# Two-layer hybrid decoder trunk on one core: activation tables loaded by name, and plain products for the last two output tiles of each FFN

## The chip, the core and the metric

The kernel runs on one core of a Trainium2 chip. TensorE multiplies, VectorE (DVE) and GpSimd (POOL) work elementwise, ScalarE (ACT) evaluates functions and copies, and SyncE (SP) starts transfers between HBM and the on-chip memory. PSUM banks hold what TensorE gives out, one bank for 128x512 numbers. The metric is the device time of one execution in microseconds (us), the median of several runs.

## What is computed

Two decoder layers work on 1024 tokens of width 1024, in float32. Each layer adds the result of an attention and then that of a gated FFN (2816 hidden columns) to its input, each behind an RMS norm; a last RMS norm ends it.

```python
def rmsnorm(x, g):
    return x * lax.rsqrt(jnp.mean(x * x, -1, keepdims=True) + EPS) * g

def swiglu(h, w_gate, w_up, w_down):
    return (jax.nn.silu(h @ w_gate) * (h @ w_up)) @ w_down

def reference(x, ...):
    for layer in range(2):
        h = rmsnorm(x, attn_norm[layer])
        x = x + (even_mixer if layer == 0 else mla_mixer)(h, ...)
        x = x + swiglu(rmsnorm(x, ffn_norm[layer]), ...)
    return rmsnorm(x, final_norm)
```

The first layer's mixer has a stick-breaking attention (its weights come from sigmoids) and a sliding-window attention (softmax); the second layer's is a latent attention (softmax) behind low-rank projections with norms of their own.

## The kernel before

Activations lie transposed: tiles of 128 features by 512 tokens, so each tensor has two token halves. Every float32 operand is split into a high and a low part (`split_w` for weights, `split_act`, `split` for activations): ScalarE copies the high part, VectorE subtracts it from the original. A product is then three matmuls of 128x128 by 128x512 (`mm3`).

**The norms.** `square_sum` collects squares of the tiles of one half in two or three partial sums (ScalarE squares; VectorE and GpSimd add). `rstd` sums them over the features with matmuls against a matrix of ones, takes Ln and Exp(-0.5 x) on ScalarE and refines the result with four operations on VectorE, the last three in a chain behind Exp. Nothing in the code says which activation table these functions use; a pass over the finished program places a table load ahead of an activation whenever the table that is loaded last does not serve it. It places one ahead of Ln, one ahead of Exp and one ahead of Silu or Sigmoid that follow.

**The FFN.** It uses seven instead of eight block products for a 2x2 block product (a fast scheme of Strassen's kind). The blocks are two halves of the features by two token halves (A, B): `FORMS` names the seven sums of activation blocks, B11, B21, T2, T1, T3, B22 and N4; B11 and B21 are blocks of half A, B22 one of half B, and T1, T2, T3, N4 are differences. `forms` loads the weight blocks and forms the matching weight sums on GpSimd (`combine`, `sub`). At the beginning of an FFN only half A's norm is at hand, so six pairs of column tiles first make the products of B11 and B21 alone (kind "plain"), gate and up in turn; Silu is applied to the first. Meanwhile half B's norm is taken, and `combinations` forms T1, T2, T3, N4 and B22 from the tiles of both halves, a piece after each product. The other products follow pair by pair (`outputs`); the four result blocks c11, c12, c21 (named u) and c22 of each pair give the forms of the down projection (`combine`), which are stored to HBM (`keep`).

The down projection runs in three chunks of 4, 4 and 3 column pairs, and within a chunk over four groups j of two output tiles each. A group has seven products of n tiles; each product's result is added to some of the four residual tiles (x11, x12, x21, x22; 11 additions and a copy in all). In the last chunk (`end`) a tile that is finished goes to `Last.add`, which squares it for the next norm and, at the end of the kernel, starts the last norm of a half as soon as its eight tiles are there. The last group of the last chunk (j == 3) uses the order `LATE`, with weight sums of kind "late"; there B's tiles are finished after the fourth and the fifth product, A's after the sixth and the seventh.

**What sets the order.** Only TensorE in the first attention is ordered by hand. Everywhere else a scheduler orders each engine's instructions by a model of times, and the engines run their queues in that order. TensorE's sums for a norm stand in its queue like any other matmul.

Of the kernel before, what the change touches and what calls it, by code (L numbers as in the profile page):

```python
# [10 lines left out]
F32 = mybir.dt.float32  # L11
# [20 lines left out]
FORMS = ("B11", "B21", "T2", "T1", "T3", "B22", "N4")  # L32
LATE = ("B11", "T2", "T1", "T3", "B22", "B21", "N4")

# [37 lines left out]
class Kernel:  # L72
# [98 lines left out]
    def forms(self, mats, twins=None):  # L171
# [3 lines left out]


        nc = self.nc
        sub = lambda o, x, y: nc.gpsimd.tensor_tensor(o, x, y, ALU.subtract)  # L178
        turns = {"fast": (0, 1, 0, 4, 2, 1, 3), "late": (0, 0, 4, 2, 0, 1, 3), "rest": (0, 4, 2, 1, 3)}
        flat = [(i, j) for i, m in enumerate(mats) for j in range(len(turns.get(m[0], m[1])))]  # L180
# [24 lines left out]
        def prep():  # L205
            i, j = flat[len(ready)]
            kind, _, n = mats[i]
            early = twins is not None and i == twins[1]
            if j == (6 if early else 0):
                for x in (i, i + 1):  # L210
                    if x < len(mats) and x not in raws:
                        load(x)
            t = raws[i]
            if kind == "rest" and j == 0:
                combine(t, n)
                sub(t[1][:, :n], t[1][:, :n], t[0][:, :n])
            ready.append(self.split_w(t[turns[kind][j] if kind in turns else j], n))
            if kind not in ("fast", "late"):
                return
            if j == (1 if kind == "fast" else 0):  # L220
                combine(t, n)
            if j == 1:
                a11, a12 = t[0][:, :n], t[1][:, :n]
                sub(a12 if kind == "fast" else a11, a12, a11)

# [39 lines left out]
    def stat_acc(self, accs, src, k):  # L265

        nc = self.nc
        out = self.tmp("acc" if len(accs) < 2 else "sq")
        if k in (1, 3, 7):
            nc.gpsimd.tensor_tensor(out, src, src, ALU.mult)  # L270
        else:
            nc.scalar.activation(out, src, AF.Square)
        if len(accs) < 2:
            accs.append(out)
            return
        eng = nc.gpsimd if k in (2, 4) else nc.vector
        eng.tensor_tensor(accs[k % 2], accs[k % 2], out, ALU.add)

    def rstd(self, r, accs, n, scale=1.0, eps=None, eps_out=None, tag="mm"):
# [67 lines left out]
    def norm_in(self, xsrc, g0, pool, tag, split=False, hook=None):  # L347
        act = [[None, None] for _ in range(NT)]
        rs = []
        for hf in range(2):  # L350
# [9 lines left out]
            if split:  # L360
                for k in range(NT):
                    self.stat_acc(accs, srcs[k], k)
            rs.append(self.rstd(self.tl(pool, [P, HALF], F32, tag, 2), accs if split else self.merge(accs), D,
                                tag="t" if split else "mm"))
# [206 lines left out]
    def swa_steps(self, mi, kbox, vbox, qbox, done):  # L571
# [4 lines left out]
        def score(b):  # L576
# [14 lines left out]
            for h in range(2):  # L591
                for i, k in enumerate((kh, kl)):
# [6 lines left out]
                                           ALU.mult, ALU.add)  # L599
            nc.vector.tensor_reduce(st, pt[:, :, o:], AX.X, ALU.max, negate=True)  # L600
            for h in range(2):
                nc.scalar.activation(pt[:, h, o:], pt[:, h, o:], AF.Exp, bias=st[:, h:h + 1],
                                     accum_out=box["s", b // 4][:, h, b % 4:b % 4 + 1])
# [323 lines left out]
    def ffn(self, layer, xt, rs, accs, first, last):  # L927
# [9 lines left out]
        add = lambda o, x, y: nc.vector.tensor_tensor(o, x, y, ALU.add)  # L937
        F = {n: [None] * 4 for n in FORMS}
        self.slot = {n: n for n in FORMS}
        NP = NHID // 2  # L940
        NA = 6
# [8 lines left out]
        def down_mat(p0, n, j):  # L950
            d = lambda m, h: dw[m][:, (h * NP + p0) * P:(h * NP + p0 + n) * P]
            kind = "late" if p0 + n == NP and j == 3 else "fast"
            return (kind, (d(2 * j, 0), d(2 * j, 1), d(2 * j + 1, 0), d(2 * j + 1, 1)), n * P)
# [68 lines left out]
        for i in range(NA):  # L1022
            for g in range(2):
                u, c = [self.tl(self.rp, [P, HALF], F32, "lone", 3) for _ in range(2)]
                nc.scalar.copy(u, p("B11"))
                keep(u, f"U{g}", i)
                add(c, u, p("B21"))
                if g == 0:
                    nc.scalar.activation(c, c, AF.Silu)
                    sil = c  # L1030
# [3 lines left out]
                if i == 0 and g == 0:  # L1034
                    rs[B] = self.rstd(self.tl(self.rp, [P, HALF], F32, "rr", 2), self.acc_list(accs[B]), D)
                    self.tctx.close()
# [7 lines left out]
        with self.pool("tc", side="right") as self.tp:  # L1044
            t = lambda tag: self.tl(self.tp, [P, HALF], F32, tag)
            def outputs(i, g, sil):
# [33 lines left out]
                add(c12, c12, p("B22"))  # L1080
                done(c12, 2)
                yield
# [42 lines left out]
        for c, (p0, n) in enumerate(chunks):  # L1125
# [4 lines left out]
            for j in range(4):  # L1130
                m1, m2 = 2 * j, 2 * j + 1
                x11, x12, x21, x22 = xt[m1][A], xt[m1][B], xt[m2][A], xt[m2][B]
                u = self.tl(self.tp, [P, HALF], F32, "u", 2)
                for name in LATE if end and j == 3 else FORMS:
                    ps = self.any_bank()
# [24 lines left out]
                    if j == 3 and not end:  # L1160
                        build(name, *chunks[c + 1], (self.tp, [P, HALF], F32, "ld", 8))

    def rope_tables(self, tp):
# [419 lines left out]
class Last:  # L1583
# [12 lines left out]
    def open(self):  # L1596
        self.ctx.callback(self.k.wctx.close)
        self.k.set_nsq(5 if self.final else 3)
        self.pool = self.k.tp = self.ctx.enter_context(self.k.pool("st", side="right"))
# [120 lines left out]
```

## Time and profile before

| | |
|---|---|
| median of 3 runs | 2467.93 us (2467.6 to 2468.2) |
| the profiled execution, its own time | 2461.47 us |
| its span, first to last instruction | 2459.7 us |
| instructions | 33726 |
| matmuls | 11242 |
| activation table loads in the built order | 35 |

The profile is of one execution. Times in its rows count from the start of its span. The page gives each engine's busy time; further views list groups of instructions by line, the busy time in stretches, and the instructions in order of time. A row in order of time gives the start, the duration, the engine, the line, the operation with output and inputs, and in brackets how long the engine sat idle before it and whose result ended that. The operations of `rstd` have lines 285 (sum), 289 (Ln behind the matmuls), 290, 296 (Exp), 297, 298 and 299.

### The profile page before, as it was taken

To read this page: it belongs to the slowest core of one execution; us is meant where nothing else is said; L and a number is where in the kernel's file an instruction comes from. 1 tells how busy PE (TensorE), PEld (TensorE's weight loads), DVE (VectorE), ACT (ScalarE), POOL (GpSimd) and SP (SyncE) were. 2 spreads that over 40 slices of the span, in tenths; PEclk is the share of its full clock that TensorE was granted. 3 is DMA by queue.
4 is the path that set the end of the run, shared out by engine and by line. 5 is a ranking of instruction groups with operands and counts; after the bars stand their busy time and mean duration, and the time that the engine had idled before them with its cause. 6 is when DMAs were issued, how large, how long until landed. Compare 5 with 4: busy or idle time off the path is not lost. (4 is left out here: it accounts for less than half of the span.)

```text
span 2459.7 us, 33726 instructions
## 1 busy us (share of the span) xinstructions
PE 2311.8 (94%) x11242; PEld 1901.9 (77%) x11242; DVE 1916.6 (78%) x2854; ACT 1229.4 (50%) x2462; POOL 975.7 (40%) x786
## 2 busy tenths in 40 slices
PE   7999999889999999999988999999889999999996
PEld 5877787777788887778666888887768888877784
DVE  7777777678577668889877888885587876788988
ACT  6555566554223334335655788774453233343453
POOL 6333323215976444333233223321035663434333
PEclk8999999999999999999999999999999999999998
DMA  3011236644354236454333111235235442354531
GB/s 130 22 39 44 66 123 202 210 137 152 116 185 150 98 105 196 141 154 133 113 117 107 50 57 53 65 134 197 86 113 171 157 166 95 107 173 144 175 104 69
DMA packets 167130, 298.65 MB, mean 121 GB/s; under 512 B 20675, under 2 KB 29356, under 8 KB 166956
## 3 DMA queue, kind: packets, MB, share of 16 engines
q1 hardware_dynamic: 166956, 296.51, 37.2%
q8 instruction: 88, 1.44, 0.2%
q14 instruction: 86, 0.70, 0.1%
HBM read 216.10 MB, written 81.38 MB: 121 GB/s over the span
## 5 line engine op out<-in xcount | busy, mean ns | idle before, releaser
L145 ACT CAST whi<-wa 128x512 fp32r<-128x512 f32 (+1 forms) x422 | 255.5, 607 | 447.1 <-PE mm L238 99.7
L146 DVE TENSOR_TENSOR wlo<-wa,whi 128x512 fp32r<-128x512 f32 (+1 forms) x422 | 344.7, 817 | 69.4 <-ACT whi L145 68.9
L178 POOL TENSOR_TENSOR wa<-s,wa 128x512 f32<-128x512 f32 (+1 forms) x66 | 93.4, 1416 | 258.8 <-DVE wlo L146 230.7
L201 POOL TENSOR_TENSOR s<-wb,wb 128x512 f32<-128x512 f32 (+1 forms) x66 | 93.8, 1421 | 200.3 <-DVE wlo L146 147.3
L1472 PE MATMUL z<-mk,mq 128*128 128x512 f32 (+2 forms) x576 | 146.9, 366 | 11.0 <-ACT w L1485 10.4
L146 DVE TENSOR_TENSOR wlo<-wb,whi 128x512 fp32r<-128x512 f32 (+1 forms) x136 | 133.6, 983 | 27.5 <-ACT whi L145 27.4
L145 ACT CAST whi<-wb 128x512 fp32r<-128x512 f32 (+1 forms) x136 | 82.3, 605 | 140.6 <-PE d L238 42.0
L1485 ACT ACTIVATE w<-z,st 128x512 f32<-128x512 f32 (+3 forms) x192 | 110.7, 582 | 35.2 <-DVE st L1481 25.3
L237 PE MATMUL mm<-hh,whi 128*128 128x512 f32 x304 | 124.2, 409 | 1.3 <-ACT whi L145 1.3
L1478 DVE TENSOR_REDUCE st<-z 128x1 f32<-128x512 f32 (+1 forms) x192 | 104.1, 550 | 25.6 <-PE z L1472 17.9
L178 POOL TENSOR_TENSOR wa<-wa,wa 128x512 f32<-128x512 f32 (+1 forms) x68 | 105.6, 1552 | 44.1 <-issue 26.9
L238 PE MATMUL mm<-hl,whi 128*128 128x512 f32 x304 | 122.4, 403 | 0.0
L239 PE MATMUL mm<-hh,wlo 128*128 128x512 f32 x304 | 121.5, 400 | 0.0
L399 DVE TENSOR_TENSOR ptl<-t,pth 128x512 fp32r<-128x512 f32 x160 | 108.1, 683 | 16.1 <-ACT pth L398 14.7
L936 POOL TENSOR_TENSOR c<-c,c 128x512 f32<-128x512 f32 x66 | 101.6, 1552 | 26.0 <-DVE c L1054 22.6
L1472 PEld LDWEIGHTS z<-mk,mq 128*128 128x128 f32 x576 | 92.7, 192 | 24.5 <-ACT w L1485 16.0
L178 POOL TENSOR_TENSOR wb<-wa,wb 128x512 f32<-128x512 f32 (+1 forms) x68 | 99.5, 1463 | 28.9 <-DMA c<-a 12.8
L398 ACT CAST pth<-t 128x512 fp32r<-128x512 f32 x160 | 91.0, 590 | 17.1 <-PE t L395 8.2
L403 PE MATMUL mm<-pth,v 128*128 128x256 f32 x320 | 93.8, 309 | 2.5 <-ACT pth L398 2.3
L395 PE MATMUL t<-ident,w 128*128 128x128 f32 x576 | 94.7, 276 | 1.3 <-ACT w L1485 1.2
L403 PE MATMUL mm<-ptl,v 128*128 128x256 f32 x320 | 87.2, 297 | 1.0 <-DVE ptl L399 1.0
L712 DVE TENSOR_TENSOR ptl<-t,pth 128x512 fp32r<-128x512 f32 x80 | 54.4, 683 | 41.9 <-ACT pth L711 41.5
(535 smaller groups left out, 7619.0 us busy)
## 6 DMA issues: line engine op xcount, KB each, us to landing
a<-c SPq DMA_DIRECT2D x120, 256.0 KB, 2.9
ld<-a SPq DMA_DIRECT2D x98, 256.0 KB, 3.4
wa<-w_gate SPq DMA_DIRECT2D x68, 256.0 KB, 2.7
wa<-w_up SPq DMA_DIRECT2D x68, 256.0 KB, 2.7
lone<-a SPq DMA_DIRECT2D x56, 256.0 KB, 3.3
wb<-w_gate SPq DMA_DIRECT2D x44, 256.0 KB, 2.9
wb<-w_up SPq DMA_DIRECT2D x44, 256.0 KB, 2.7
wa<-w_in SPq DMA_DIRECT2D x36, 256.0 KB, 2.6
```

What stands on the lines that cost most here:

```text
L145: nc.scalar.copy(hi[:, :n], raw[:, :n])
L146: nc.vector.tensor_tensor(lo[:, :n], raw[:, :n], f(hi[:, :n]), ALU.subtract)
L178: sub = lambda o, x, y: nc.gpsimd.tensor_tensor(o, x, y, ALU.subtract)
L237: mm(ps, wh, xh, start=first, stop=False)
L238: mm(ps, wh, xl, start=False, stop=False)
L239: mm(ps, wl, xh, start=False, stop=last)
L399: nc.vector.tensor_tensor(lo, t, f(hi), ALU.subtract)
L403: nc.tensor.matmul(o[:, :256], vs, pt[:, j * 256:(j + 1) * 256], start=(kb == kb0 and j == 0 and i == 0), stop=(kb == NB - 2 and j == 1 an ...
L936: sub = lambda o, x, y: nc.gpsimd.tensor_tensor(o, x, y, ALU.subtract)
L1472: nc.tensor.matmul(z[:, :wd + ext], qq[:, q0:q0 + P], kk[:, k0 - ext:k0 + wd], start=y == 0, stop=y == 2 and x > 0)
L1478: nc.vector.tensor_reduce(st[:, x:x + 1], zs[x], AX.X, ALU.max, negate=True)
L1485: nc.scalar.activation(w[:, o:o + wd], zs[x], AF.Exp, bias=st[:, 2 * np_ - 2:2 * np_ - 1], accum_out=box[p]["s"][c // 2][:, 8 * x + j:8 * ...
```

## The change

It has two parts.

First, a new function `ln_exp` loads one named table that holds Ln, Exp and the copies, and is pinned to its place in ScalarE's program order. It is called at the first half of the first norm, at the first step of the sliding-window attention, and at the beginning of each FFN's last chunk (`Last.open`). So that Silu doesn't come between, half B's norm is written ahead of the first Silu of the FFN, and this Silu is pinned too.

Second, in each FFN's last chunk the two output tiles of the last group are formed without the fast scheme: four outputs (two tiles, two halves), each from two products that accumulate in one bank, first half B's two tiles, then half A's. That takes the block c12 as a form of its own, "B12". For the three column pairs of the last chunk it is stored to HBM and, in the group before, after that group's product with T1, fetched into the place of T2's low parts and split into the place of T1. The order `LATE` and the weight sums of kind "late" are gone; the weights of that group are loaded as they are.

```diff
+    def ln_exp(self):
+        self.tc.keep_in_program_order(self.nc.scalar.preload_act_table_set("natural_log_exp_and_others"))
...
-            kind = "late" if p0 + n == NP and j == 3 else "fast"
+            kind = "plain" if p0 + n == NP and j == 3 else "fast"
...
                 add(c, u, p("B21"))
+                if i == 0 and g == 0:
+                    rs[B] = self.rstd(self.tl(self.rp, [P, HALF], F32, "rr", 2), self.acc_list(accs[B]), D)
                 if g == 0:
-                    nc.scalar.activation(c, c, AF.Silu)
+                    silu = nc.scalar.activation(c, c, AF.Silu)
+                    if i == 0:
+                        self.tc.keep_in_program_order(silu)
...
                 add(c12, c12, p("B22"))
-                done(c12, 2)
+                done(c12, 2, "B12" if i >= chunks[-1][0] else None)
...
+                if end and j == 3:
+                    w = [take() for _ in range(4)]
+                    for hf, top, bottom, m, x, r in (
+                            (B, "B12", "B22", m1, x12, 0), (B, "B12", "B22", m2, x22, 2),
+                            (A, "B11", "B21", m1, x11, 0), (A, "B11", "B21", m2, x21, 2)):
+                        ps = self.any_bank()
+                        self.prod(ps, w[r], F[top], n, True, False)
+                        self.prod(ps, w[r + 1], F[bottom], n, False, True)
+                        add(x, x, ps)
+                        fin(m, hf)
+                    continue
...
+                    if j == 2 and end and name == "T1":
+                        for k in range(n):
+                            F["B12"][k] = self.form_tile("B12", k)
+                            self.split(fetch(self.tl(self.fm, [P, HALF], F32, f"T2l{k}"), "B12", p0 + k), F["B12"][k])
...
     def open(self):
         self.ctx.callback(self.k.wctx.close)
+        self.k.ln_exp()
```

How the instructions stand on the engines now: at the beginning of layer 0's FFN, on ScalarE, before (the line 1029 is Silu, `rr` is half B's norm).

```order
L1025 COPY lone_5717<-d_5719 128x512
L1029 ACT_TABLE_LOAD
L1029 ACTIVATE lone_5633<-lone_5633 128x512
L289 ACT_TABLE_LOAD
L289 ACTIVATE sq_5706<-mm_5703,eps_70 128x512
L296 ACT_TABLE_LOAD
L296 ACTIVATE rr_5701<-sq_5706 128x512
L145 CAST whi_5777<-wa_5681 128x512
```

The same place now (lines 1028 and 1034 are the copy and Silu).

```order
L1028 COPY lone_5719<-d_5721 128x512
L287 ACTIVATE sq_5707<-mm_5704,eps_70 128x512
L294 ACTIVATE rr_5702<-sq_5707 128x512
L1034 ACT_TABLE_LOAD
L1034 ACTIVATE lone_5635<-lone_5635 128x512
L144 CAST whi_5779<-wa_5683 128x512
```

Two of the three loads are gone, and the norm's two functions have moved ahead of Silu.

At the end of the kernel, on TensorE, before: the end of the sixth product of the last group (bank d), the sums of half B (lines 285), and the seventh product, with N4.

```order
L239 MATMUL d_23904<-B21h_23201,wlo_23844 128x512
L285 MATMUL mm_23893<-acc_23500,ones_62 128x512
L285 MATMUL mm_23893<-sq_23889,ones_62 128x512
L237 MATMUL mm_23918<-N4h_23386,whi_23859 128x512
L238 MATMUL mm_23918<-N4l_23387,whi_23859 128x512
L239 MATMUL mm_23918<-N4h_23386,wlo_23860 128x512
```

Now, in the fourth output (bank b, half A's second tile), from its second matmul to its eleventh; lines 283 are the sums of half B.

```order
L232 MATMUL b_23921<-B11l_23167,whi_23819 128x512
L283 MATMUL mm_23887<-acc_23514,ones_62 128x512
L233 MATMUL b_23921<-B11h_23166,wlo_23820 128x512
L231 MATMUL b_23921<-B11h_23172,whi_23819 128x512
L232 MATMUL b_23921<-B11l_23173,whi_23819 128x512
L233 MATMUL b_23921<-B11h_23172,wlo_23820 128x512
L231 MATMUL b_23921<-B11h_23178,whi_23819 128x512
L232 MATMUL b_23921<-B11l_23179,whi_23819 128x512
L233 MATMUL b_23921<-B11h_23178,wlo_23820 128x512
L231 MATMUL b_23921<-B21h_23202,whi_23836 128x512
L283 MATMUL mm_23887<-sq_23883,ones_62 128x512
L232 MATMUL b_23921<-B21l_23203,whi_23836 128x512
```

Half B's sums have moved from ahead of the last product of nine into the last output of eighteen; eight more of its matmuls follow the last sum.

At the end of layer 0's FFN, on TensorE, before: the last matmul of the last product, the sums, and the first matmuls of the latent attention's first two groups (banks t and z).

```order
L239 MATMUL b_11648<-N4h_11147,wlo_11603 128x512
L285 MATMUL mm_11825<-acc_11248,ones_62 128x512
L285 MATMUL mm_11825<-sq_11632,ones_62 128x512
L237 MATMUL t_11799<-hh_12895_11677,whi_11741 128x512
L237 MATMUL z_11897<-hh_12895_11677,whi_11753 128x512
L285 MATMUL mm_11838<-acc_11189,ones_62 128x512
```

The same place now.

```order
L233 MATMUL d_11646<-B21h_10958,wlo_11575 128x512
L283 MATMUL mm_11832<-acc_11257,ones_62 128x512
L283 MATMUL mm_11832<-sq_11621,ones_62 128x512
L283 MATMUL mm_11845<-acc_11198,ones_62 128x512
L231 MATMUL t_11806<-hh_12896_11684,whi_11748 128x512
L231 MATMUL z_11904<-hh_12896_11684,whi_11760 128x512
```

The sums stand behind the last product as before; they are now of tiles that were finished two outputs earlier, and the third stands ahead of the next stage's first matmul.

## Rows read from the trace of the kernel before

**Rows 1.** The page, part 1: busy time, share of the span, number of instructions.

```profile
PE 2311.8 (94%) x11242; PEld 1901.9 (77%) x11242; DVE 1916.6 (78%) x2854; ACT 1229.4 (50%) x2462; POOL 975.7 (40%) x786
```

**Rows 2.** Stretches of 60 us: length; busy PE, PEld, DVE, ACT, POOL; clock; DMA.

```profile
540.00:600.00 60.00, 54.00 (x229) 42.11 (x228) 51.77 (x67) 35.10 (x58) 20.95 (x12) 1.00 0.43 140
600.00:660.00 60.00, 55.14 (x229) 44.35 (x228) 31.18 (x46) 15.16 (x27) 56.20 (x70) 0.94 0.42 138
...
1200.00:1260.00 60.00, 52.52 (x221) 40.22 (x220) 46.38 (x70) 39.76 (x61) 17.31 (x15) 1.00 0.28 88
...
1800.00:1860.00 60.00, 53.77 (x231) 42.30 (x230) 54.21 (x67) 30.48 (x55) 26.83 (x17) 1.00 0.46 154
...
1920.00:1980.00 60.00, 60.00 (x266) 49.67 (x266) 46.34 (x56) 16.43 (x28) 38.60 (x27) 1.00 0.53 178
```

**Rows 3.** Groups by line, ScalarE: count, busy us, mean ns, idle before.

```profile
L296 ACT ACT_TABLE_LOAD x14 | 18.0, 1283 | 0.3
...
L289 ACT ACT_TABLE_LOAD x10 | 12.8, 1283 | 1.2 <-PE mm L285 1.1
```

**Rows 4.** In order of time, 40 to 57 us: ScalarE, VectorE, TensorE.

```profile
40.88 1.28 ACT L289 ACT_TABLE_LOAD   x1
...
44.84 1.51 DVE L297 TENSOR_TENSOR w<-r 128x512 f32<-128x512 f32 x1 [0.96 <-ACT r L296]
...
56.33 3.34 PE L688 MATMUL z<-qk,qk 128*128 128x256 f32 x8 [4.79 <-POOL qk L525]
```

**Rows 5.** In order of time, 540 to 598 us: TensorE, ScalarE, VectorE.

```profile
540.76 1.02 PE L285 MATMUL mm<-acc,ones 128*128 128x512 f32 x2
...
541.84 1.28 ACT L1029 ACT_TABLE_LOAD   x1
...
545.08 0.69 ACT L289 ACTIVATE sq<-mm,eps 128x512 f32<-128x512 f32 x1
545.79 1.28 ACT L296 ACT_TABLE_LOAD   x1
547.08 0.63 ACT L296 ACTIVATE rr<-sq 128x512 f32<-128x512 f32 x1
...
545.80 0.69 DVE L290 TENSOR_SCALAR sq<-mm 128x512 f32<-128x512 f32 x1 [3.56 <-ACT sq L289]
547.75 0.69 DVE L297 TENSOR_TENSOR sq<-rr 128x512 f32<-128x512 f32 x1 [1.25 <-ACT rr L296]
...
597.35 0.69 DVE L146 TENSOR_TENSOR wlo<-wa,whi 128x512 fp32r<-128x512 f32 x1 [0.61 <-ACT whi L145]
```

**Rows 6.** In order of time, 1220 to 1310 us, VectorE: first and last of four.

```profile
1228.44 0.69 DVE L297 TENSOR_TENSOR sq<-rkv 128x512 f32<-128x512 f32 x1 [1.28 <-ACT rkv L296]
...
1302.73 0.69 DVE L297 TENSOR_TENSOR sq<-rq 128x512 f32<-128x512 f32 x1 [2.73 <-ACT rq L296]
```

**Rows 7.** In order of time, 1175 to 1199 us, TensorE: end of layer 0.

```profile
1175.20 0.39 PE L237 MATMUL mm<-B11h,whi 128*128 128x512 f32 x1
...
1192.87 2.08 PE L285 MATMUL mm<-acc,ones 128*128 128x512 f32 x2 [3.23 <-DVE x L937]
...
1198.98 0.39 PE L239 MATMUL t<-hh,wlo 128*128 128x512 f32 x1
```

**Rows 8.** In order of time, 2415 to 2460 us: TensorE, then VectorE.

```profile
2415.67 0.39 PE L237 MATMUL b<-B11h,whi 128*128 128x512 f32 x1
...
2430.09 1.51 PE L285 MATMUL mm<-acc,ones 128*128 128x512 f32 x2 [2.02 <-DVE acc L912]
...
2435.43 0.39 PE L239 MATMUL mm<-N4h,wlo 128*128 128x512 f32 x1
...
2436.00 0.69 DVE L297 TENSOR_TENSOR sq<-rf 128x512 f32<-128x512 f32 x1 [1.25 <-ACT rf L296]
...
2448.82 6.51 DVE L1624 SCALAR_TENSOR_TENSOR x<-x,gains,rf 128x512 f32<-128x512 f32 x5
```

**Rows 9.** The page, part 6: issues, KB each, us from issue to landing.

```profile
a<-c SPq DMA_DIRECT2D x120, 256.0 KB, 2.9
```

More of the change, by code (lines that the diff above doesn't have):

```diff
@@ L32 @@
 FORMS = ("B11", "B21", "T2", "T1", "T3", "B22", "N4")
-LATE = ("B11", "T2", "T1", "T3", "B22", "B21", "N4")
 def f(ap):
@@ L178, in forms @@
         sub = lambda o, x, y: nc.gpsimd.tensor_tensor(o, x, y, ALU.subtract)
-        turns = {"fast": (0, 1, 0, 4, 2, 1, 3), "late": (0, 0, 4, 2, 0, 1, 3), "rest": (0, 4, 2, 1, 3)}
+        turns = {"fast": (0, 1, 0, 4, 2, 1, 3), "rest": (0, 4, 2, 1, 3)}
         flat = [(i, j) for i, m in enumerate(mats) for j in range(len(turns.get(m[0], m[1])))]
@@ L217, in prep @@
             ready.append(self.split_w(t[turns[kind][j] if kind in turns else j], n))
-            if kind not in ("fast", "late"):
-                return
-            if j == (1 if kind == "fast" else 0):
+            if kind == "fast" and j == 1:
                 combine(t, n)
-            if j == 1:
-                a11, a12 = t[0][:, :n], t[1][:, :n]
-                sub(a12 if kind == "fast" else a11, a12, a11)
+                sub(t[1][:, :n], t[1][:, :n], t[0][:, :n])
         def take():
@@ L362, in norm_in @@
                     self.stat_acc(accs, srcs[k], k)
+            if hf == 0:
+                self.ln_exp()
             rs.append(self.rstd(self.tl(pool, [P, HALF], F32, tag, 2), accs if split else self.merge(accs), D,
@@ L600, in score @@
             nc.vector.tensor_reduce(st, pt[:, :, o:], AX.X, ALU.max, negate=True)
+            if mi == b == 0:
+                self.ln_exp()
             for h in range(2):
@@ L937, in ffn @@
         add = lambda o, x, y: nc.vector.tensor_tensor(o, x, y, ALU.add)
-        F = {n: [None] * 4 for n in FORMS}
+        F = {n: [None] * 4 for n in FORMS + ("B12",)}
         self.slot = {n: n for n in FORMS}
+        self.slot["B12"] = "T1"
         NP = NHID // 2
@@ L1034, in ffn @@
                 if i == 0 and g == 0:
-                    rs[B] = self.rstd(self.tl(self.rp, [P, HALF], F32, "rr", 2), self.acc_list(accs[B]), D)
                     self.tctx.close()
@@ L1132, in ffn @@
                 x11, x12, x21, x22 = xt[m1][A], xt[m1][B], xt[m2][A], xt[m2][B]
+                if end and j == 3:
[9 more added lines that the diff above has]
+                    continue
                 u = self.tl(self.tp, [P, HALF], F32, "u", 2)
-                for name in LATE if end and j == 3 else FORMS:
+                for name in FORMS:
                     ps = self.any_bank()
```

## The prediction

> **What bounds the kernel now.** The page comes first: TensorE is busy for 94% of the span [rows 1], so a gain must take away matmuls or one of its waits. The table by stretches says where those waits are: none from 1920 to 1980 us, where 266 matmuls fill 60.00 us (0.2256 us each), but 6.0 us between 540 and 600, 6.2 between 1800 and 1860, 7.5 between 1200 and 1260 [rows 2]. Then ScalarE's groups: a table load takes 1283 ns and stands 24 times at the Ln and Exp of the norms alone [rows 3]; the built order has 35 in all, the changed one 8. Removed: 27 x 1.283 = 34.6 us of ScalarE. That engine is not the bound, so each load is priced where it stands, by who waits behind it, from the timelines of the start, of an FFN's beginning, of the latent attention's projections and of the two places where an FFN ends.
>
> **Loads at the start.** The second half's norm goes load, Ln, load, Exp, VectorE, and TensorE waits 4.79 us for what comes of it [rows 4]. The two loads are 2.57 us. But VectorE had been idle only 0.96 us when the Exp came, so the rest may be its own queue, whose order is a little different now. Gain 0.5 to 2.6; I take 1.5, nearer to the 0.96. A load that is new in this place stands ahead of the first half's last split; VectorE's own queue is later there, and I cost it at nothing. Without that cover it takes 1.28 back, and the lower end would be -0.8.
>
> **Loads at each FFN's beginning.** A load for Silu, one for Ln, one for Exp follow from 541.84 on. VectorE waits 3.56 us before the first operation of the norm and 1.25 before the second, which starts at 547.75 [rows 5]. In the new order Ln and Exp stand where the first load stood: Ln to 542.5, Exp to 543.2, so that second operation starts 4.5 us earlier, and with it the sums and splits of the other half's blocks. From there VectorE has no gap until 597.35 [rows 5], and TensorE waits for it, 6.0 us in that stretch [rows 2]; up to 4.5 of them can come back. Silu pays: it stands behind Exp and its load, and ends near 545.1. What it is multiplied with takes two more products, which hides that; without that cover it costs under 2 us. Bounds 0 and 4.5. In layer 0 the stretch from 600 to 660 has another 4.9 us of waits [rows 2] while GpSimd forms the position tables, and these could take some back: I take 2.5 there. In layer 1, where no tables are formed, 3.5.
>
> What a load costs is where the Trainium skill speaks otherwise: the page "ScalarE: Activation LUTs", section "What ACT_TABLE_LOAD costs", adds a drain of 1.38 us to the 1.283. The rows show none: the load of 545.79 ends at 547.07 and Exp starts at 547.08 [rows 5]. By the page the 27 loads would be 71.8 us of ScalarE, by the rows 34.6; the sum goes by the rows.
>
> **Loads in the latent attention's projections.** Eight loads go, in four norms. VectorE waits for the Exp of each of the last four: 1.28 us at 1228.44, 2.73 at 1302.73, two more between [rows 6]. At least the load between Ln and Exp is on each chain, 4 x 1.283 = 5.1; TensorE's waits are 7.5 us in the first 60 us of the stage [rows 2]. Some of them belong to neighbours, such as a weight split in VectorE's queue. Bounds 0 and 7.5; I take 4.5, nearer to one load per chain.
>
> **The FFN's last group.** Seven combined products of 9 matmuls become four outputs of 18: 72 instead of 63, so 9 x 0.2256 = 2.03 us more in each layer, 4.06 if paid in full. Removed: four GpSimd operations, three weight splits, a copy, and 7 of VectorE's 11 additions; added: three fetches and three splits. At 0.69 for an operation of 128x512 [rows 5] VectorE has (7 - 3) x 0.69 = 2.8 us less, and the three shorter weight splits beside it. The fetches go on SP's queue among the last weight loads; they may start when the third pair of tiles has used the same buffers, 36 matmuls or 8.1 us before the group, and a transfer of this size takes 2.9 [rows 9]. I cost them at nothing; if one came late the group would start late by what is missing, at most 3.
>
> At the end of layer 0 the group starts at 1175.20; after it TensorE waits 3.23 us for VectorE, which is still adding; the sums then run slowly (2.08 us for a pair that takes 1.02 at 540.76 [rows 5]), and the fourth matmul of the next stage starts at 1198.98, 23.8 us after the group's start [rows 7]. In the new order the half that the next stage needs is finished after 36 of the 72 matmuls, and the sums stand behind all of them: 75 matmuls, 16.9, and three sums at 1.02, together 20.0 with no wait. That gives 3.8, the added matmuls included. VectorE's 16 splits bound what comes later; I take 3.5, with bounds -2.03 (matmuls added, no wait removed) and 3.8.
>
> At the kernel's end the group starts at 2415.67 and its last product ends at 2435.82, with a wait of 2.02 us and two slow sums inside [rows 8]: 20.15 us. Now 72 matmuls and two sums: 16.24 + 2.04 = 18.3; gain 1.9. Behind it VectorE runs from 2436.00 without a gap worth naming: the first half's norm, five scalings, 6.5 us, the second half's norm, five scalings to 2455.33 [rows 8]. It stays the bound. Its start is Ln, load and Exp behind the first half's sums; these now end eight matmuls (1.8 us) ahead of the last product, and Ln and Exp (0.69 and 0.63 [rows 5], no load) follow, so that VectorE starts some 0.4 us before the product's end instead of 0.18 after. Together 1.9 + 0.6 = 2.5, bounds -1 and 4.
>
> **A cost that the trace doesn't show.** In the last three column pairs one more block is stored, and a subtraction on GpSimd that overwrites it must wait until the store has landed: 2.9 us [rows 9], with sums of weights queued behind it, and ScalarE, VectorE and TensorE behind those. Six times 2.9 is 17.4 at worst, nothing at best; a gain has no reason. GpSimd is busy for 38.60 of 60 us in a stretch of this kind [rows 2]; so I take 0 and keep 3 for the range.
>
> **The sum** against the profiled execution (its own time 2461.47): 1.5 + 2.5 + 3.5 + 4.5 + 3.5 + 2.5 = 18.0, which gives 2443.5. The median of the runs, 2467.93, is 6.5 above that execution; carried over, 2449.9.
>
> **Rivals.** First, the loads are hidden: VectorE's queue is the bound at every norm, and what ScalarE gains is waited out elsewhere. Then the two last groups count, 6.0, and the start, 1.5: 2460.4. For it: VectorE without a gap in most of these stretches. Against it: its waits name Ln and Exp [rows 5, 6].
>
> Second, slower: the two groups pay and get nothing back. TensorE does 18 more matmuls, 4.06 us; the first half's sums are not ready ahead of the last product, the next stage's splits and the scalings start behind it as before, and the loads are hidden by the same queue: 2472. It decides as soon as VectorE ends the first half's additions later than the last nine matmuls start. Against it: these sums stand nineteen and ten rows ahead of the end in the new order, and VectorE has less to do.
>
> Third, the stores: if GpSimd's queue is just in time, two thirds of the 17.4 come on top of the forecast, 2461.5. Against it: GpSimd's idle time.
>
> Fourth, a load costs more than its row: if each held back what follows by as much again, the load terms (12.0 us) would double, 2437.9. The Trainium skill's page "ScalarE: Activation LUTs" has a drain of that kind. Against it: the Exp that starts as the load ends [rows 5].
>
> **How the numbers follow.** Forecast 0.60, hidden loads 0.18, stores 0.08, dear loads 0.08, unpaid groups 0.06. With its own terms at their nearer ends the forecast reaches from about 2441 to 2458; the range takes in the hidden loads and the stores, 2440 to 2462, and leaves out the dear loads and the unpaid groups, 0.14. About 0.2%, 5 us, is what a measurement can tell from no change. Faster by more: the forecast, the dear loads, most of the hidden loads and the stores, 0.88; within: 0.07, where these two give a few us less; slower: 0.05.
>
> **What would show it.** Eight load rows instead of 35; TensorE idle for near 3 us from 540 to 600, and near 2 to 3 after 1800; VectorE's first operations of a norm with no load ahead; no wait ahead of the sums behind layer 0's last product, and about 1 us for each; the first half's five scalings just behind the last product of all. I am wrong if TensorE's waits in these stretches stay as they were or move into the next one (600 to 660 above all), or if GpSimd's subtractions late in each FFN grow a wait for the store.

## The result

The changed kernel took 2445.79 us (median of 5 runs, 2444.12 to 2448.54), the kernel before 2467.93 on the same chip (2467.37 to 2468.85): ratio 0.9912, 95% interval 0.9898 to 0.9925, 22.1 us faster. Forecast were 2449.9 us and a range from 2440 to 2462. The profiled execution took 2448.54 us, span 2446.8.

### The profile after

The page's first part, which answers to [rows 1], shows TensorE at 95%, with 18 rows more, and ScalarE 33 us less busy:

```profile
PE 2315.0 (95%) x11260; PEld 1907.8 (78%) x11260; DVE 1910.4 (78%) x2840; ACT 1196.3 (49%) x2433; POOL 970.5 (40%) x778
```

ScalarE's table loads, by line (count, busy us, mean ns, idle before), are 8 where there were 35. They answer to [rows 3]:

```profile
L275 ACT ACT_TABLE_LOAD x4 | 5.1, 1283 | 0.1
L1034 ACT ACT_TABLE_LOAD x2 | 2.6, 1283 | 0.0
L144 ACT ACT_TABLE_LOAD x1 | 1.3, 1283 | 0.7 <-PEq L1734 0.7
L692 ACT ACT_TABLE_LOAD x1 | 1.3, 1283 | 0.0
```

The same stretches of 60 us as in [rows 2] (length; busy PE, PEld, DVE, ACT, POOL; clock; DMA):

```profile
540.00:600.00 60.00, 56.77 (x237) 44.53 (x236) 54.91 (x72) 31.89 (x56) 24.17 (x12) 0.98 0.42 134
600.00:660.00 60.00, 57.22 (x244) 46.66 (x243) 34.31 (x45) 15.08 (x27) 54.49 (x69) 0.97 0.43 143
1200.00:1260.00 60.00, 56.09 (x240) 44.00 (x239) 53.03 (x81) 34.29 (x61) 17.25 (x15) 1.00 0.33 100
1800.00:1860.00 60.00, 56.72 (x243) 44.74 (x242) 53.20 (x67) 28.06 (x50) 31.26 (x19) 1.00 0.48 157
```

TensorE's waits there are 3.2 us (6.0 before), 2.8 (4.9), 3.9 (7.5) and 3.3 (6.2).

The beginning of the first FFN in order of time (TensorE's sums, then ScalarE, then VectorE) answers to [rows 5]. Ln and Exp stand ahead of Silu's load, and the norm's second operation on VectorE starts 549.93 - 547.43 = 2.50 us behind the sums, where it was 547.75 - 540.76 = 6.99: 4.49 earlier, as worked out (4.5).

```profile
547.43 1.02 PE L283 MATMUL mm<-acc,ones 128*128 128x512 f32 x2
...
548.54 0.69 ACT L287 ACTIVATE sq<-mm,eps 128x512 f32<-128x512 f32 x1
549.26 0.63 ACT L294 ACTIVATE rr<-sq 128x512 f32<-128x512 f32 x1
549.91 1.28 ACT L1034 ACT_TABLE_LOAD   x1
...
549.93 0.69 DVE L295 TENSOR_TENSOR sq<-rr 128x512 f32<-128x512 f32 x1
```

The four norms of the latent attention, VectorE's operation behind Exp, answer to [rows 6], whose two middle rows are these:

```profile
1247.56 0.69 DVE L297 TENSOR_TENSOR sq<-rq 128x512 f32<-128x512 f32 x1 [2.73 <-ACT rq L296]
1283.90 0.69 DVE L297 TENSOR_TENSOR sq<-rkv 128x512 f32<-128x512 f32 x1 [2.65 <-ACT rkv L296]
```

The waits were 1.28, 2.73, 2.65 and 2.73 us; they are 5.0 us less together, and one load per norm is 4 x 1.283 = 5.1. In the changed kernel:

```profile
1226.01 1.23 DVE L295 TENSOR_TENSOR sq<-rkv 128x512 f32<-128x512 f32 x1 [0.76 <-ACT rkv L294]
1243.02 0.69 DVE L295 TENSOR_TENSOR sq<-rq 128x512 f32<-128x512 f32 x1 [1.46 <-ACT rq L294]
1277.62 0.69 DVE L295 TENSOR_TENSOR sq<-rkv 128x512 f32<-128x512 f32 x1 [0.70 <-ACT rkv L294]
1295.42 0.69 DVE L295 TENSOR_TENSOR sq<-rq 128x512 f32<-128x512 f32 x1 [1.46 <-ACT rq L294]
```

The end of layer 0 on TensorE answers to [rows 7]: the last group starts, the sums stand behind its 72 matmuls without a wait and take 1.02 us each, and the first matmul of the next stage by the weights' low part follows 19.59 us behind the start (23.78 before). `T1h` in these rows is the place that the block B12 now has.

```profile
1179.22 0.39 PE L231 MATMUL mm<-T1h,whi 128*128 128x512 f32 x1
...
1195.55 1.02 PE L283 MATMUL mm<-acc,ones 128*128 128x512 f32 x2
1196.41 1.02 PE L283 MATMUL mm<-sq,ones 128*128 128x512 f32 x2
1197.27 1.02 PE L283 MATMUL mm<-acc,ones 128*128 128x512 f32 x2
...
1198.81 0.40 PE L233 MATMUL t<-hh,wlo 128*128 128x512 f32 x1
```

The kernel's end, TensorE and then VectorE, answers to [rows 8]:

```profile
2404.58 0.39 PE L231 MATMUL d<-T1h,whi 128*128 128x512 f32 x1
...
2422.47 0.39 PE L233 MATMUL b<-B21h,wlo 128*128 128x512 f32 x1
...
2422.50 0.69 DVE L295 TENSOR_TENSOR sq<-rf 128x512 f32<-128x512 f32 x1
...
2426.11 6.52 DVE L1647 SCALAR_TENSOR_TENSOR x<-x,gains,rf 128x512 f32<-128x512 f32 x5
...
2435.32 6.51 DVE L1647 SCALAR_TENSOR_TENSOR x<-x,gains,rf 128x512 f32<-128x512 f32 x5
```

### Where the time went, stretch by stretch

The spans of the two profiled executions differ by 12.9 us only, the medians by 22.1. To see why, each execution is cut at the starts of the same matmuls on TensorE. Three more executions stand beside: a second one of each kernel, and the second part of the change alone, whose order is that of before, instruction for instruction, until well into the first FFN. All in us.

| from, to | before | before, again | changed | changed, again | second part alone |
|---|---|---|---|---|---|
| start to first score | 56.33 | 56.37 | 55.83 | 56.16 | 56.63 |
| to the sliding attention | 280.14 | 280.96 | 280.19 | 280.45 | 280.55 |
| to the output projection | 140.75 | 144.14 | 147.40 | 147.12 | 148.45 |
| to the first FFN's first product | 47.29 | 47.29 | 48.40 | 46.82 | 47.30 |
| to its first T2 product | 82.34 | 81.72 | 78.62 | 78.50 | 82.33 |
| to its last group | 568.34 | 568.73 | 568.79 | 566.88 | 568.41 |
| to the next stage's first low product | 23.79 | 22.46 | 19.59 | 19.59 | 19.59 |
| to the latent attention's first score | 82.01 | 84.52 | 77.65 | 77.66 | 87.14 |
| to the second FFN's first product | 494.69 | 497.24 | 492.11 | 493.15 | 496.38 |
| to its first T2 product | 81.36 | 81.52 | 78.23 | 78.72 | 81.81 |
| to its last group | 558.63 | 557.72 | 557.79 | 557.99 | 557.11 |
| to its last product's end | 20.14 | 18.49 | 18.28 | 18.28 | 18.28 |
| to the end | 23.86 | 24.31 | 23.89 | 23.90 | 26.82 |
| span | 2459.68 | 2465.48 | 2446.76 | 2445.23 | 2470.79 |

One stretch, the sliding attention, takes 140.75 to 148.45 us in three executions of one and the same order. In the first trace of before it was at its shortest. VectorE waits there for a bias that is fetched from memory, but that does not explain the lengths: these waits come to 13.6, 13.6 and 15.6 us in before, before again, and the second part alone, so they differ by 2.0 us where the stretch differs by 7.7. What makes the stretch long in one execution and short in another is not shown.

Where a stretch is compared below, it is one that does not vary like this.

### The profile page after: what moved, and what is told of

Same layout as the page of the kernel before. It is cut to its first block, busy times and chain, and to the rows that moved or that the text cites. A ratio compares the mean times of both kernels' runs of the same rounds, so it can differ in the third digit from the quotient of the medians.

```text
span 2446.8 us, 33748 instructions
## 1 busy us (share of the span) xinstructions
PE 2315.0 (95%) x11260; PEld 1907.8 (78%) x11260; DVE 1910.4 (78%) x2840; ACT 1196.3 (49%) x2433; POOL 970.5 (40%) x778
## 4 chain that ended last, share of the span: by engine, by line
PE 70%; DVE 14%; issue 4%; DMA 4%; ACT 3%; POOL 3%; SPq 0%; DVEq 0%; POOLq 0%; ACTq 0%
PE mm L231 7%; PE mm L232 7%; PE mm L233 7%; PE b L233 4%; PE a L233 4%; PE a L232 4%; PE d L233 4%; PE a L231 4%; PE b L232 4%; PE z L1494 4%; PE b L231 4%; PE d L232 4%; PE d L231 4%; PE mm L403 3%; DVE wlo L145 2%
## 5 line engine op out<-in xcount | busy, mean ns | idle before, releaser
L399 DVE TENSOR_TENSOR ptl<-t,pth 128x512 fp32r<-128x512 f32 x160 | 108.3, 683 | 15.6 <-ACT pth L398 14.3
L938 POOL TENSOR_TENSOR c<-c,c 128x512 f32<-128x512 f32 x66 | 101.5, 1550 | 26.1 <-DVE c L1060 22.7
L882 POOL TENSOR_TENSOR acc<-acc,sq 128x512 f32<-128x512 f32 x26 | 35.8, 1375 | 143.5 <-ACT sq L877 143.4
```

Of the source, the lines that this page charges most:

```text
L399: nc.vector.tensor_tensor(lo, t, f(hi), ALU.subtract)
```

## The experiments

### Before and changed, once more

Both kernels as they are.

> The kernel before, unchanged, for a second profile. Between the trace of before and that of the changed kernel one stretch that the prediction does not name lost 7.8 us: from the sliding attention (matmul at 336.48 before, 336.02 after) to the FFN's first product (524.52 and 531.82). Theory A: that stretch hangs on transfers that go to memory and back, and its length differs between executions of the same kernel; this run then shows some 190 to 196 us for it, where the first profile had 188.0, and a span 2 to 8 us above 2459.7. Theory B: the change itself costs 7.8 us there by its new order; this run then shows 188.0 again, within 1 us.

Before: 2467.25 us, span 2465.5, and 144.14 us for the sliding attention, 191.4 up to the FFN's first product. That is theory A: it is longer than in the first execution though nothing was changed. That transfers to memory are the reason, as theory A says, is not shown by this run.

> The changed kernel, unchanged, beside the kernel before on one chip: a second profile and a second ratio. Theory A: the gain by the times is 18 to 23 us, and the stretch from the sliding attention to the FFN's first product is as long as in the second profile of before, within 2 us. Theory B: this stretch takes 195.8 us again and is 7 to 8 us longer than in the second profile of before; the gain by the times is then only that of the other stretches.

Changed: 2447.01 us against 2468.96 of before on the same chip (17 runs, 2464.25 to 2475.35), ratio 0.9909 (0.9894 to 0.9925), 22 us again. The stretch is 193.9, which is 2.5 longer than in the second execution of before; A asked for 2. A small part of the difference may belong to the order; eight executions in the new order took 143.0 to 147.4 for the sliding attention, three in the old 140.8 to 148.5, so it can't be told.

### The first part alone

The kernel before with the three calls that load the table by name (in `norm_in`, at the sliding attention's first Exp, and in `Last.open`) and with the norm ahead of the first Silu; the last group stays at seven combined products.

```
+            if hf == 0:
+                self.ln_exp()
...
+            if mi == b == 0:
+                self.ln_exp()
...
+                if i == 0 and g == 0:
+                    rs[B] = self.rstd(self.tl(self.rp, [P, HALF], F32, "rr", 2), self.acc_list(accs[B]), D)
                 if g == 0:
...
+        self.k.ln_exp()
```

> The first part alone: the table loaded by name, and the norm ahead of the first Silu in each FFN; the last group stays with its seven combined products. The forecast's terms that belong to it: start 1.5, the FFNs' beginnings 2.5 + 3.5, the latent attention's projections 4.5, together 12.0 us, and 0.6 at the kernel's end, so about 2455. The rival of hidden loads: 1.5 us alone, about 2466. The rival of dear loads: 24 us, about 2444.

2452.33 us against 2468.96: ratio 0.9936 (0.9921 to 0.9951), 16 us faster; 12.6 had been forecast for it. Its stretches: first FFN's beginning 78.56, last group of layer 0 to the first score 22.65 + 78.94 = 101.59, second FFN's beginning 79.03, last group to the end 20.11 + 22.63 = 42.74. From the first score of the latent attention to the second FFN it takes 491.85 us, where before took 494.69 and 497.24; no term of the forecast stood there, and it makes up what is above the 12.6. The hidden loads (1.5 us) fall, and the dear loads (24 us) too.

### The second part alone

The changed kernel with the same pieces taken out again.

```
-            if hf == 0:
-                self.ln_exp()
...
-            if mi == b == 0:
-                self.ln_exp()
...
-                if i == 0 and g == 0:
-                    rs[B] = self.rstd(self.tl(self.rp, [P, HALF], F32, "rr", 2), self.acc_list(accs[B]), D)
                 if g == 0:
...
                 if i == 0 and g == 0:
+                    rs[B] = self.rstd(self.tl(self.rp, [P, HALF], F32, "rr", 2), self.acc_list(accs[B]), D)
...
-        self.k.ln_exp()
```

> The second part alone: plain products, one half first, in each FFN's last group; every Ln and Exp keeps its own table load. The forecast: 3.5 us at the end of layer 0 and 1.9 at the kernel's end (the other 0.6 there needs the missing load), so 5.4 us, about 2462.5. The rival of unpaid groups: 18 matmuls more and no wait less, 4 us slower, about 2472. If the two parts help each other, their gains alone add up to less than that of both.

2472.01 against 2468.96: ratio 1.0007 (0.9996 to 1.0018). No gain. The group at the end of layer 0 itself became as short as in the changed kernel (19.59), but the next stretch grew to 87.14, and the two together took 106.73, where before took 105.80 and 106.98. At the kernel's end the 18.28 us were there too, and the rest took 26.82, 2.9 more than in the changed kernel. ScalarE there:

```profile
2442.20 1.28 ACT L283 ACT_TABLE_LOAD   x1 [5.83 <-PE mm L279]
2443.49 0.69 ACT L283 ACTIVATE sq<-mm,eps 128x512 f32<-128x512 f32 x1
2444.20 1.28 ACT L290 ACT_TABLE_LOAD   x1
2445.49 0.63 ACT L290 ACTIVATE rf<-sq 128x512 f32<-128x512 f32 x1
```

Both loads stand behind the sums, 2.57 us on the path. The parts were forecast at 12.6 and 5.4 us, each by itself; by the runs they are 16 and nothing: the second part's gain exists only where the loads are gone.

### One call less

```
     def open(self):
         self.ctx.callback(self.k.wctx.close)
-        self.k.ln_exp()
```

> The changed kernel without the load by name at the opening of the last sums (one call out of three places): from the end of layer 0 on every Ln and Exp has its own load again, in the four norms of the latent attention, at the second FFN's beginning and at the kernel's end; both last groups stay plain. Stretches of the changed kernel in two executions: last group of layer 0 to the first score of the latent attention 97.2; second FFN's start to its first T2 product 78.2 and 78.7; last group to the end 42.2. Theory A (the loads in the norms' chain are what ends these stretches, so that without the named table the plain group's gain is waited out behind them): 106 to 107 us, 80 to 81, and 45, that is 9 + 2 + 3 us more, as in the run of the second part alone. Theory B (the two parts' gains simply add up): the first stretch grows by what the table alone gave there, 5 us, to 102, and the last by under 1 us.

2465.09 against 2471.32 (9 runs of before on the same chip): ratio 0.9971 (0.9959 to 0.9984). The three stretches took 19.59 + 87.41 = 107.0, 81.83, and 18.28 + 26.48 = 44.8: theory A in all three, the second 0.8 above its range. VectorE at two of the four norms, with waits of 2.7 us again:

```profile
1229.63 0.69 DVE L295 TENSOR_TENSOR sq<-rkv 128x512 f32<-128x512 f32 x1 [2.69 <-ACT rkv L294]
...
1248.81 0.69 DVE L295 TENSOR_TENSOR sq<-rq 128x512 f32<-128x512 f32 x1 [2.73 <-ACT rq L294]
```

With the plain group, the loads from there to the first score cost 107.0 - 97.2 = 9.8 us. With the combined group they cost 106.4 (mean of the two executions of before) - 101.6 = 4.8. And the plain group gains 101.6 - 97.2 = 4.4 without loads, and 0 with them: a stage that waits for a chain of norms swallows what the stage ahead of it gives.

### The other half first

```
-                            (B, "B12", "B22", m1, x12, 0), (B, "B12", "B22", m2, x22, 2),
-                            (A, "B11", "B21", m1, x11, 0), (A, "B11", "B21", m2, x21, 2)):
+                            (A, "B11", "B21", m1, x11, 0), (A, "B11", "B21", m2, x21, 2),
+                            (B, "B12", "B22", m1, x12, 0), (B, "B12", "B22", m2, x22, 2)):
```

> The changed kernel with the halves of the two last groups in the other order: the half whose norm and sums the next stage starts with comes second. If the order of the halves is what takes the wait out of the end of layer 0, the stretch from the group's start to the next stage's first matmul by the weights' low part goes from 19.6 back to 22 to 23.5 us, and at the kernel's end the stretch from the group's start to the end grows by 2 to 4 us over 42.2, since the scalings then start behind the last addition and a norm. If plain products alone do it, both stay within 0.5 us.

2447.90 against 2471.32: ratio 0.9907 (0.9892 to 0.9921), the changed kernel's. Group to the next stage's first low product 19.87 (19.59), last group to the end 42.27 (42.2). The plain products alone took the wait out of the group. Two things limit this run. At the kernel's end the exchange is symmetric: here half A is finished first, its sums stand inside the last output, and its scalings come first, so the run can't tell there what it is worth to finish one half first. And at the end of layer 0 the order is worth something, though not in the group: the next stretch takes 78.64 us (77.65 in the changed kernel), and from the group to the first score it is 98.50 against 97.24.

### The norm behind Silu

```
-                if i == 0 and g == 0:
-                    rs[B] = self.rstd(self.tl(self.rp, [P, HALF], F32, "rr", 2), self.acc_list(accs[B]), D)
                 if g == 0:
                     silu = nc.scalar.activation(c, c, AF.Silu)
...
                 if i == 0 and g == 0:
+                    self.ln_exp()
+                    rs[B] = self.rstd(self.tl(self.rp, [P, HALF], F32, "rr", 2), self.acc_list(accs[B]), D)
```

> The changed kernel with the norm behind the first Silu again in each FFN, as before, but with the table for Ln and Exp still loaded by name ahead of it: Silu's load, Silu, the named load, Ln, Exp. The norm's second operation on VectorE starts 2.5 us behind the sums in the changed kernel and 7.0 in the kernel before; here 1.28 + 0.65 + 1.28 later than in the changed one, about 5.5. If VectorE's start is what sets the stretch from the FFN's first product to its first T2 product (78.5 changed, 82.0 before), it is about 80.5 to 81 in both layers, so that half of the gain came from the order and half from the loads. If only the number of loads matters, it stays below 79.5.

2448.81 against 2471.32: ratio 0.9910 (0.9895 to 0.9925). The stretches took 79.97 and 79.36, where the changed kernel has 78.5 and 78.2 to 78.7. TensorE's sums and VectorE's second operation of the norm:

```profile
544.22 1.02 PE L283 MATMUL mm<-acc,ones 128*128 128x512 f32 x2
...
551.08 0.68 DVE L295 TENSOR_TENSOR sq<-rr 128x512 f32<-128x512 f32 x1
```

That operation starts 6.86 us behind the sums, nearly as late as before (6.99) and not 5.5: a product's addition and a weight split stand ahead of it in VectorE's queue. Yet only 1.4 and some 0.9 us of the gain are lost. My expectation is missed: VectorE's start explains under half of the 3.5 and 3.0 us. The number of loads does not explain them either. This version and the kernel with one call less both have three loads at the second FFN's beginning (four before, one in the changed kernel), and the one with Ln and Exp first, each with a load, gains nothing there (81.83). What goes with the length there, if roughly, is how long VectorE is idle. These are the second FFN's stretches of before, of one call less, of this version and of the changed kernel's second execution (length; busy PE, PEld, DVE, ACT, POOL; clock; DMA):

```profile
1775.69:1857.05 81.36, 70.95 (x291) 55.23 (x291) 67.79 (x90) 42.67 (x71) 25.25 (x15) 0.96 0.38 126
```

```profile
1780.57:1862.40 81.83, 72.44 (x290) 55.89 (x291) 70.52 (x92) 43.02 (x73) 28.04 (x17) 0.94 0.40 133
```

```profile
1770.91:1850.27 79.36, 71.84 (x290) 55.75 (x291) 70.41 (x91) 42.51 (x71) 24.37 (x15) 0.94 0.40 133
```

```profile
1766.34:1845.06 78.72, 70.44 (x290) 55.18 (x291) 69.91 (x92) 40.67 (x71) 24.29 (x16) 0.96 0.41 136
```

VectorE is idle for 13.6, 11.3, 8.9 and 8.8 us: with the norm behind Silu it works on its queue while it waits for Exp. In the first FFN this does not separate the versions (11.2 us idle here, 11.3 and 11.0 in the changed kernel), so which wait decides stays open.

### GpSimd's part of the last scalings on VectorE

```
-                    nc.gpsimd.tensor_tensor(xs[i], xs[i], r, ALU.mult)
+                    nc.vector.tensor_tensor(xs[i], xs[i], r, ALU.mult)
```

> The changed kernel with the last three of the eight scalings of each half on VectorE too, not on GpSimd. The five that stand on VectorE take 1.30 us each while GpSimd multiplies, and the same kind of operation takes 0.67 to 0.75 where GpSimd is idle. If GpSimd's work is what slows them, eight of them take 8 x 0.73 = 5.8 us instead of 6.5 for five, and the stretch from the last product's end to the kernel's end falls from 23.9 to about 22.5; if they are slow by themselves, eight take 10.4 and the end comes 7 to 8 us later.

2442.64 against 2471.32: ratio 0.9881 (0.9866 to 0.9896). The last product's end to the kernel's end: 20.60 us instead of 23.90, more than expected. VectorE's eight scalings of the first half, from 2421.99 to 2427.20, are done in 5.2 us, where five took 6.52:

```profile
2421.99 0.69 DVE L1645 TENSOR_TENSOR x<-x,rf 128x512 f32<-128x512 f32 x1
2422.60 0.75 DVE L1647 SCALAR_TENSOR_TENSOR x<-x,gains,rf 128x512 f32<-128x512 f32 x1
...
2425.13 2.07 DVE L1647 SCALAR_TENSOR_TENSOR x<-x,gains,rf 128x512 f32<-128x512 f32 x3
```

### The FFN's first subtractions on VectorE too

On top of the version just shown: `sub` is GpSimd's.

```
-            sub(t1, h12, raw["B11"][k])
+            nc.vector.tensor_tensor(t1, h12, raw["B11"][k], ALU.subtract)
...
-            sub(t2, h22, t1)
+            nc.vector.tensor_tensor(t2, h22, t1, ALU.subtract)
...
-            sub(n4, raw["B21"][k], t2)
+            nc.vector.tensor_tensor(n4, raw["B21"][k], t2, ALU.subtract)
```

> The version with all last scalings on VectorE, and besides the 12 subtractions of each FFN's beginning that form the combined blocks of the second half (GpSimd, 1.6 to 2.2 us each) on VectorE too. There VectorE's operations on SBUF take up to 1.78 us beside GpSimd's, 0.69 alone. If GpSimd's company costs VectorE more than the subtraction itself (0.69), the stretch from the FFN's first product to its first T2 product falls from 78.3 and 77.9 by 1 to 3 us in each layer, and the kernel to 2437 to 2441. If the company costs about what the subtraction costs, both stretches stay within 0.5 us and the kernel at about 2442.6. If VectorE's queue was the bound by its count of operations alone, they grow by 3 to 8 us.

2431.67 against 2471.97: ratio 0.9839 (0.9824 to 0.9853), 40 us under before and 11 under the version ahead of it, twice what the best case gave. The two stretches fell from 78.28 and 77.88 to 73.21 and 73.85, by 5.1 and 4.0 where 1 to 3 had been expected. TensorE has no wait left in the stretches of 60 us there:

```profile
540.00:600.00 60.00, 60.00 (x265) 49.30 (x264) 55.13 (x86) 36.95 (x64) 8.34 (x4) 1.00 0.54 171
600.00:660.00 60.00, 60.00 (x266) 49.69 (x265) 40.32 (x55) 17.64 (x30) 57.14 (x72) 1.00 0.41 132
1800.00:1860.00 60.00, 60.00 (x267) 49.67 (x266) 50.70 (x71) 26.35 (x45) 19.99 (x14) 1.00 0.47 154
```

VectorE carries 12 operations more in each FFN's beginning, and its busy time there does not grow (67.15 and 66.90 us in the first FFN, 70.27 and 67.41 in the second), since its others are no longer held up. A second cause is not separated from this one: the subtractions themselves are quicker, and what follows them starts earlier. ScalarE waited 11.3 us for GpSimd's subtractions in the first FFN's stretch of the version ahead, and for none of them here. The same split of a block in the changed kernel, and in this one:

```profile
559.23 1.78 DVE L927 TENSOR_TENSOR T1l<-hb,T1h 128x512 fp32r<-128x512 f32 x1
```

```profile
555.34 0.69 DVE L927 TENSOR_TENSOR T1l<-hb,T1h 128x512 fp32r<-128x512 f32 x1
```

This version beats both kernels.

## Why the prediction was right, and where it was not

The forecast was of the right sign and 4.1 us too slow. It reads 24 loads at the norms' Ln and Exp; there are 28, since the Ln of the latent norms has a line of its own, and the 35 in all and the 27 removed are right. Term by term, with the mean of two executions of each kernel:

**Start: 1.5 forecast, 0.35 measured**, below its lower bound. The mis-sized step is "nearer to the 0.96": VectorE's first operation of the norm starts 2.13 us earlier (42.71, [rows 4] has 44.84), but the two behind it now fall beside GpSimd and take 1.66 and 1.67 us instead of 0.69 each, and the score starts 0.50 earlier only. VectorE before, these two, and then the three in the changed kernel:

```profile
46.38 0.69 DVE L298 SCALAR_TENSOR_TENSOR w<-w,w 128x512 f32<-128x512 f32 x1
47.11 0.69 DVE L299 SCALAR_TENSOR_TENSOR r<-w,r 128x512 f32<-128x512 f32 x1
```

```profile
42.71 1.18 DVE L295 TENSOR_TENSOR w<-r 128x512 f32<-128x512 f32 x1
43.93 1.66 DVE L296 SCALAR_TENSOR_TENSOR w<-w,w 128x512 f32<-128x512 f32 x1
45.62 1.67 DVE L297 SCALAR_TENSOR_TENSOR r<-w,r 128x512 f32<-128x512 f32 x1
```

GpSimd in the same execution:

```profile
43.42 3.33 POOL L525 TENSOR_TENSOR qk<-ev,qk 64x512 fp32r<-64x512 f32 x2
```

**FFN's beginnings: 2.5 + 3.5 forecast, 3.5 + 3.0 measured** (82.03 to 78.56, 81.44 to 78.48). The sum is right. The argument was only half right: VectorE's earlier start was forecast to the tenth, but the norm behind Silu shows that this start carries a minor part. What carries the rest stays open.

**Latent attention's loads: 4.5 forecast, 5.6 measured up to the first score** (83.27 to 77.66), and 3.3 more behind it. Two of the four norms stand behind the first score (1283.90 and 1302.73; the score starts at 1280.99), and from there to the second FFN the stretch is 3.3 us shorter (495.97 to 492.63). By all traces that belongs to the loads: the last score starts 394.9 to 397.8 us behind the first in the four executions with a load for each Ln and Exp there, and 391.7 to 393.7 in the seven without. Together that is 8.9 us, above the bound of 7.5. The term was sized by VectorE's waits for four Exps, which did lose 5.0 us; four loads of the norm ahead of the projections (1202.54 to 1210.71) stood in no term. How the 8.9 us divide among the loads is not shown.

**End of layer 0: 3.5 forecast, 3.5 measured** (23.13 to 19.59; 20.0 forecast for the changed stretch). Two steps of it were wrong all the same. The half that comes first plays no part in the group (19.87 us with the halves exchanged). And the gain was costed as if it were the group's own: alone it is 0, since the norms behind it were waiting for their loads anyway. The forecast added the terms; it is right only because both parts are there.

**Kernel's end: 2.5 forecast, 1.2 measured** (43.40 to 42.18), within its bounds. The group's own 18.3 us came out (18.28), and VectorE's norm started 0.4 us ahead of the last product's end, as worked out. But the wait of 2.02 us that was to go was shorter in the second execution of before (18.49 for the group). And the 0.6 us behind the product were gained and lost again: VectorE's last scaling ends 19.0 us behind the last product, where it was 19.5 and 20.0, but from there to the kernel's end it takes 4.92 us instead of 4.34 and 4.35. Why, no run shows. The sign "the first half's five scalings just behind the last product" failed: an addition, a merge of sums and the norm's own operations lie between, and they start 3.2 us behind it (3.8 and 4.2 before).

**Stores on GpSimd: 0 forecast.** Its late subtractions wait as before (26.1 us in all for their main group, 26.0 before), and with the change none of them waits longer for a store: one waits 2.4 us for it in both kernels.

Together these terms give 17.2 us of the 18.0 forecast, and 20.5 with the stretch behind the latent attention's first score. That the sum comes near the medians' 22.1 is in part luck: the start and the kernel's end were 2.4 us too high, the latent attention 4.4 too low. Over the whole, these four executions differ by 16.6 us only (2462.6 to 2446.0), since the sliding attention, where nothing was forecast, took 4.8 us more in the two changed ones; the other stretches give 0.9. The first trace of before caught its sliding attention 3.4 us shorter than the second, and the carry-over to the median, 6.5 us, took this in without knowing it. Whether the new order lengthens the sliding attention stays open.

**The rivals.** Hidden loads: the first part alone gains 16 us, not 1.5. But not every load was on a path: the sums of the norm ahead of the second FFN stand 35.37 us ahead of its first product in every trace, with two loads behind them or none. Unpaid groups: wrong for the change as a whole, but this is what the second part does by itself, 1.0007. Stores: no wait that the change adds. Dear loads: the first part alone gains 16 us, not 24, and by the rows Exp starts as the load ends (2444.20 + 1.28 and 2445.49). By the Trainium skill ("ScalarE: Activation LUTs", section "What ACT_TABLE_LOAD costs") a drain of 1.38 us comes with it; no run here shows one.

## What to carry to other kernels

Price a table load by the chain it stands in: where TensorE has other work until the norm is done, it costs nothing; in a chain of norms that TensorE waits for it costs up to its whole 1.28 us, and there it can also swallow what the stage ahead of it gains. Test the parts of a change one at a time, since a gain of nothing alone can be 4 us behind another. And before work is given to GpSimd to relieve VectorE, look at how long VectorE's neighbours take beside it: here 24 subtractions and 6 multiplications taken back by VectorE took 15 to 18 us more off, beside the change's 22.

## What the hardware showed beside

VectorE's operations of 128x512 with both operands in SBUF (tensor-tensor) take 0.68 us on average where GpSimd is idle for over nine tenths of their time (607 of them in the changed kernel's second trace), 1.25 where it works for over four fifths (some 215), and 1.80 at most. With one operand in PSUM it is 0.68 either way (some 550 and 240). The Trainium skill, "SBUF — State Buffer", section "SBUF: two separate sides", has a port pair that the two engines take in turn, a VectorE operation with two SBUF inputs among those that need it; the trace agrees. At the kernel's end, without GpSimd's company, 2.6 of the 3.3 us gained lie between VectorE's first scaling and its last (15.72 to 13.10); the 5.1 and 4.0 us at the FFNs' beginnings hold the quicker subtractions as well.

A table load is not always made ahead of a wait. At the kernel's end of the kernel before, the load of the first norm ran while ScalarE had nothing to do, and Ln waited 2.94 us for the sums behind it. With the second part alone that load itself waited 5.83 us for the same sums, though ScalarE was idle. What decides between the two, these runs don't show. ScalarE before:

```profile
2429.12 1.28 ACT L289 ACT_TABLE_LOAD   x1
2433.34 0.69 ACT L289 ACTIVATE sq<-mm,eps 128x512 f32<-128x512 f32 x1 [2.94 <-PE mm L285]
```
